# Two activation splits of the second feed-forward, queued behind the third copy of the next pair

## The chip, the cores and the metric

The kernel runs on one core of one Trainium2 chip. The metric is the device time of one execution in microseconds; the time of a kernel is the median of several runs. Shorter is better. TensorE is called PE below, VectorE DVE, ScalarE ACT, GpSimd POOL and SyncE SP, as the profile names them.

## The reference

The reference is one decoder layer on 512 tokens of width 1024. What the change touches is its last sub-layer, a gated feed-forward of width 2816:

```python
def swiglu(x, w_gate, w_up, w_down):
    return (jax.nn.silu(x @ w_gate) * (x @ w_up)) @ w_down

    f = swiglu(rms_norm(h, ffn2_norm_pre[l]), ffn2_w_gate[l], ffn2_w_up[l], ffn2_w_down[l])
    h = h + 0.5 * rms_norm(f, ffn2_norm_post[l])
```

The same feed-forward stands at the layer's beginning with other weights; between the two lie attention, a gated linear recurrence and an output product. All of it is float32.

## The kernel before

**Two halves of each number.** Every float32 operand of a product is split into a high and a low float32r part: ACT writes the high part (`split`, L302), DVE subtracts it from the source for the low part (L303). A product is then three matmuls, high by high, high by low and low by high (L729 to L731, in `seventh`). So each split is one ACT instruction and one DVE instruction that waits for it.

**Pairs and seven products.** The 2816 columns of gate and up are 22 blocks of 128. A pair is gate and up of one block. From block 3 on a pair is made by seven products of half-size matrices instead of eight (a Strassen-Winograd scheme); each product is 12 matmuls of 256 columns, so a pair is 84 matmuls. `seven_on` runs the products in the order p1, p5, p6, p2, p7, p3, p4 and sums on top of each other in PSUM: p6 is added onto p1 in the same bank `b`, p7 onto that. Between them the partial sum must be copied out of `b`, since the next product overwrites it. The copies are ACT instructions (`copy`, L743). There are four in a pair: the first after p1, the second (`c5`) after p5, the third (`c6`) after p6, and the fourth after p7. p7 may not write `b` until the third copy has read it, and p4 may not start until the fourth has written the bank that p4 adds to. The block's activation is then silu(gate) times up (L966 and L953 on ACT, L952, L957 and L962 on DVE).

**Parts.** Four blocks make a part. `into` gathers a part's four activations in the tile `tt` (one buffer), and makes the seven combinations that the product with the down weights needs; each is split into an `xf` tile, of which there are four buffers. At the fourth block of a part DVE forms the remaining sums in place in `tt` (L921, L927, L928), and four splits are made: p7, p5, then one of 1024 columns for p6 and p4 together, then one of 1024 columns for p2 and p3 together. These last two are what the change touches. The product of the part with the down weights (`down7`, L1046 to L1048) is done in four steps, one behind each of the next four pairs: p1 and p7, then p4 and p6, then p5, then p2 and p3.

**Order of the work.** The five engines run their own queues, each in its order. The order in a queue comes from a scheduler that goes by the order of the code and by priorities: work under `high_priority(offset=AHEAD)` (100) is put ahead of plain work, and work under `offset=EVAC` (200), such as the copies, ahead of that. `issue_after` keeps an instruction behind a named one. The splits of the next weights (`w_forms`, L691 to L696 for its sums, and `d_forms`, L988 to L1002) are made under `AHEAD` too, on the same two engines. Weights come by DMA from SP's queue into four `raw` buffers, each freed by the DVE subtraction that reads it last.

The second feed-forward has the parts of blocks 0 to 3, 4 to 7, 8 to 11 and 12 to 15, and a last one of six blocks without such splits. So the last splits of parts 1, 2 and 3 fall in the pairs of blocks 8, 12 and 16, all run by `seven_on`, and those of part 0 in the pair of block 4, run by the older form `seven`.

Of the kernel before, what the change touches and what calls it, by code (L numbers as in the profile page):

```python
# [12 lines left out]
AF = mybir.ActivationFunctionType  # L13
# [17 lines left out]
HB = 256  # L31
# [4 lines left out]
AHEAD = 100  # L36
# [147 lines left out]
def hybrid_layer(ctx: ExitStack, tc: tile.TileContext, xT: bass.AP, xN: bass.AP, wst: bass.AP,  # L184
                 first: bass.AP, rows: bass.AP, consts: bass.AP, bias: bass.AP, out: bass.AP):
    nc = tc.nc
    DVE, ACT, PE = nc.vector, nc.scalar, nc.tensor
# [44 lines left out]
    state = {"g": 0, "i": 0, "off": 0, "raw": None, "ahead": AHEAD, "split": None}  # L232
# [68 lines left out]
    def split(dh, dl, src):  # L301
        state["split"] = ACT.activation(dh, src, AF.Copy).ins  # L302
        state["low"] = DVE.tensor_sub(dl, src, dh.bitcast(F32)).ins  # L303

    def acc_ps():
        return psum.tile([P, T], F32, name="acc", tag="acc", bufs=5)
# [4 lines left out]
    def tmp(name):  # L311
        return tpool.tile([P, T], F32, name=name, tag="t")
# [39 lines left out]
    HALVES = (slice(0, HB), slice(HB, T))  # L352
# [369 lines left out]
    def seventh(t, w, p, ps, start):  # L722
        at = t[p].at
        if len(at(0, 0).shape) == 3:
            ps = ps.rearrange("q (b t) -> q b t", b=2)
        for k in range(4):
            ks = slice(k * P, (k + 1) * P)
            wh, wl, xh, xl = w[p][:, 0, ks], w[p][:, 1, ks], at(0, k), at(1, k)
            PE.matmul(ps, wh, xh, start=start and k == 0, stop=False, skip_group_check=True)  # L729
            PE.matmul(ps, wh, xl, start=False, stop=False, skip_group_check=True)  # L730
            state["product"] = PE.matmul(ps, wl, xh, start=False, stop=k == 3, skip_group_check=True).ins  # L731

    def seven_on(t, w, g0, g1, u0, u1):

        b, z, y, v = (acc_ps()[:, :HB] for _ in range(4))

        def copy(ps, dst=None):
            if dst is None:  # L740
                dst = tpool.tile([P, HB], F32, name="c", tag="c", bufs=CB)
            with tc.high_priority(offset=EVAC):
                state["copied"] = ACT.activation(dst, ps, AF.Copy).ins  # L743
            return dst

        seventh(t, w, "p1", b, True)
        copy(b, y)
        seventh(t, w, "p5", z, True)
        c5 = copy(z)
        seventh(t, w, "p6", b, False)  # L750
        c6 = copy(b)
        seventh(t, w, "p2", y, False)
        g0(y)
        seventh(t, w, "p7", b, False)
        copy(b, v)
        state["kept"] = state["copied"]
        u1(b, c5)
        seventh(t, w, "p3", z, False)
        g1(z, c6)
        seventh(t, w, "p4", v, False)  # L760
        u0(v)
# [62 lines left out]
        product("p4", o, False)  # L824
        fold(o, u[0], sign)

    def seven(t, w, z, g, u):


        b, y = acc_ps()[:, :HB], acc_ps()[:, :HB]  # L830

        def product(p, ps, start):
            seventh(t, w, p, ps, start)

        def copy(ps):
            c = tpool.tile([P, HB], F32, name="c", tag="c", bufs=CB)
            with tc.high_priority(offset=EVAC):
                ACT.activation(c, ps, AF.Copy)
            return c

        def sum_of(dst, ps, c):
            with tc.high_priority(offset=EVAC):
                DVE.tensor_add(dst, ps, c)

        product("p1", b, True)
        c1 = copy(b)
        product("p2", y, True)
        sum_of(g[0], y, c1)
        product("p6", b, False)
        c6 = copy(b)  # L850
        product("p5", z, True)
        c5 = copy(z)
        product("p7", b, False)
        c7 = copy(b)
        sum_of(u[1], c7, c5)
        product("p4", y, True)
        sum_of(u[0], y, c7)
        product("p3", z, False)
        sum_of(g[1], z, c6)

    def ffn(n, x, r, forms_x, apool, pss):
        t, steps = forms_x
        acts, sevens = {}, {}

        def f32r_big():
            return apool.tile([P, 4, T], F32R, name="xf", tag="xf", bufs=4)
# [1 line left out]
        def part_of(f):  # L868
            return next(a for a, (f0, f1) in enumerate(FF_PARTS) if f < f1)

        def act_at(f):

            a = part_of(f)
            i = f - FF_PARTS[a][0]
            if i == 0:
                acts[a] = apool.tile([P, 4, T], F32R, name="act4", tag="tt", bufs=1)
            elif i % 2 == 0:
                acts[a] = f32r_big()
            at, i = acts[a], i % 2
            acts["at", f] = at[:, 2 * i, :], at[:, 2 * i + 1, :]  # L880
            return acts["at", f]
# [7 lines left out]
        def into(f, put):  # L889

            a = part_of(f)
            if a not in SEVEN:
                u = tmp("u")
                put(u, lambda ap: ap)
                split(*act_at(f), u)
                return
            i = f - FF_PARTS[a][0]
            if i == 0:
                sevens[a] = {"tt": apool.tile([P, 4, 2, HB], F32, name="tt", tag="tt", bufs=1)}
            x = sevens[a]  # L900
            tt = x["tt"]
            put(tt[:, i // 2 * 2:i // 2 * 2 + 2, i % 2, :], lambda ap: ap.rearrange("p (q t) -> p q t", q=2))
            q = tt.rearrange("p q j t -> p q (j t)")

            def pair(*ps):
                v = f32r_big().rearrange("p (s c) t -> p s (c t)", s=2)
                for k, p in enumerate(ps):
                    x[p] = v[:, :, k * T:k * T + T]
                return v

            def form(v, src):
                split(v[:, 0], v[:, 1], src)


            if i == (1 if a else 3):
                pair("p1", "p7")
                form(x["p1"], q[:, 0])
                DVE.tensor_sub(q[:, 0], q[:, 0], q[:, 1])
            if i == 3:
                with tc.high_priority(offset=AHEAD):  # L920
                    DVE.tensor_sub(q[:, 1], q[:, 3], q[:, 1])  # L921
                    form(x["p7"], q[:, 1])
                    two = pair("p6", "p4")
                    v = f32r_big().rearrange("p c t -> p (c t)")
                    x["p5"] = v[:, 0:2 * T].rearrange("p (s t) -> p s t", s=2)
                    form(x["p5"], q[:, 0])
                    DVE.scalar_tensor_tensor(q[:, 0], q[:, 3], -1.0, q[:, 0], op0=ALU.mult, op1=ALU.subtract)  # L927
                    DVE.scalar_tensor_tensor(q[:, 1], q[:, 0], -1.0, q[:, 2], op0=ALU.mult, op1=ALU.subtract)  # L928
                    form(two, tt[:, 0:2].rearrange("p q j t -> p (q j t)"))
                    form(pair("p2", "p3"), tt[:, 2:4].rearrange("p q j t -> p (q j t)"))  # L930

        def std_out(psg, psu, f):

# [11 lines left out]
        def prod(f, w):  # L945
            g, u = tmp("g"), tmp("u")
            if f >= FIRST_ON[n]:
                lo, hi = HALVES

                def g1(z, c6):  # L950
                    with tc.high_priority(offset=EVAC):
                        DVE.tensor_add(g[:, hi], z, c6)  # L952
                    ACT.activation(g[:, hi], g[:, hi], AF.Silu)  # L953

                def u1(b, c5):
                    with tc.high_priority(offset=EVAC):
                        DVE.tensor_add(u[:, hi], b, c5)  # L957

                def u0(v):
                    def put(dst, view):  # L960
                        for q, (h, src) in enumerate(zip(HALVES, (v, u[:, hi]))):
                            DVE.scalar_tensor_tensor(dst[:, q] if len(dst.shape) == 3 else dst[:, h], g[:, h], -1.0,  # L962
                                                     src, op0=ALU.mult, op1=ALU.mult)
                    into(f, put)

                seven_on(t, w, lambda y: ACT.activation(g[:, lo], y, AF.Silu), g1, u0, u1)  # L966
                return
            seven(t, w, acc_ps()[:, :HB], [g[:, h] for h in HALVES], [u[:, h] for h in HALVES])
            ACT.activation(g, g, AF.Silu)
            into(f, lambda dst, v: DVE.scalar_tensor_tensor(dst, v(g), -1.0, v(u), op0=ALU.mult, op1=ALU.mult))  # L970

# [101 lines left out]
        for ev in ffn_order(n):  # L1073
            if ev[0] == "std":
                j = ev[1]
# [46 lines left out]
    u1 = act_of(*act_two(ap1))  # L1122
# [10 lines left out]
    for k in range(KC):  # L1133
        wh, wl, raw = wts[k]
        if k == 0:

            z = hm(0)
# [74 lines left out]
    with ExitStack() as mx:  # L1212
# [38 lines left out]
        def values_two(steps, then):  # L1251
# [78 lines left out]
            for j in range(2):  # L1330
# [4 lines left out]
        t, steps = forms_of(lambda i, j: Form(lambda s, k: um_t[2 * i + k // 2][:, s, k % 2, HALVES[j]]),  # L1335
                            apool, False, rec_half)
# [160 lines left out]
        two = []  # L1497
# [7 lines left out]
        for c in range(0, KC, 2):  # L1505
            g, u = tmp("g"), tmp("u")
            seven_wide(t, pair_of(("pair", 52 + c, 53 + c)), [g[:, h] for h in HALVES], [u[:, h] for h in HALVES],
                       then=gate)
# [3 lines left out]
        for c in range(KC):  # L1512
            ps = acc_ps()
            if c % 2 == 0:
                two = fetch(("attn", c))
# [3 lines left out]
    with ExitStack() as mx:  # L1519
# [151 lines left out]
        for i, (what, hd) in enumerate(LRU_ORDER):  # L1671
# [9 lines left out]
            def then():  # L1681
                if i + 1 < len(LRU_ORDER):
                    prepare(LRU_ORDER[i + 1])
# [189 lines left out]
```

## Time and profile before

| what | us |
|---|---|
| median of 3 runs | 1208.86 (1208.83 to 1209.17) |
| profiled execution, its own time | 1210.52 |
| its span, first to last instruction | 1208.7 |
| PE busy in it | 1200.0 |
| DVE busy in it | 1033.3 |
| ACT busy in it | 832.6 |

The pairs by seven products of the second feed-forward run from 899.7 to 1169.3 us of the span. A row of the chain or of the timeline begins with the start in us from the span's start, and the duration in us; the engine, the line of the kernel, and the tiles written and read follow. `x2` is a count of equal instructions in a row; a bracket at the end is the engine's idle time before, and what ended it. Matmuls and ACT and DVE instructions are pipelined: the next can start a little before the one before it has ended, so what an instruction costs its queue is the distance from its start to the next start.

### The profile page before, as it was taken

To read this page: it belongs to the slowest core of one execution; us is meant where nothing else is said; L and a number is where in the kernel's file an instruction comes from. 1 tells how busy PE (TensorE), PEld (TensorE's weight loads), DVE (VectorE), ACT (ScalarE), POOL (GpSimd) and SP (SyncE) were. 2 spreads that over 40 slices of the span, in tenths; PEclk is the share of its full clock that TensorE was granted. 3 is DMA by queue.
4 is the path that set the end of the run, shared out by engine and by line. 5 is a ranking of instruction groups with operands and counts; after the bars stand their busy time and mean duration, and the time that the engine had idled before them with its cause. 6 is when DMAs were issued, how large, how long until landed. Compare 5 with 4: busy or idle time off the path is not lost.

```text
span 1208.7 us, 18872 instructions
## 1 busy us (share of the span) xinstructions
PE 1200.0 (99%) x7222; PEld 1070.1 (89%) x7222; DVE 1033.3 (85%) x1626; ACT 832.6 (69%) x1447; POOL 26.1 (2%) x51
## 2 busy tenths in 40 slices
PE   9999999999999999999999999999999999999997
PEld 8889999999888888888888888888899999999996
DVE  7999888889689899999868899874898888889964
ACT  6566787887566576767736988734566677778763
POOL 0000000000011000000000000000100000000000
PEclk9999999999999999999999999999999999999999
DMA  7224343434625232222323432235443333343441
GB/s 267 88 92 124 135 139 106 140 111 153 247 102 163 71 97 96 88 75 92 111 66 120 163 122 99 85 108 191 141 140 105 123 123 124 121 128 118 140 175 70
DMA packets 45819, 149.77 MB, mean 124 GB/s; under 512 B 5152, under 2 KB 8608, under 8 KB 45728
## 3 DMA queue, kind: packets, MB, share of 16 engines
q1 hardware_dynamic: 38160, 131.09, 32.9%
q0 software_dynamic: 7280, 17.30, 4.3%
q8 instruction: 56, 0.92, 0.3%
q14 instruction: 35, 0.29, 0.1%
q10 hardware_dynamic: 288, 0.17, 0.0%
HBM read 138.06 MB, written 6.29 MB: 119 GB/s over the span
## 4 chain that ended last, share of the span: by engine, by line
PE 91%; DVE 4%; ACT 3%; issue 1%; DMA 1%; DVEq 0%; ACTq 0%
PE acc L729 9%; PE acc L780 9%; PE acc L731 9%; PE acc L730 9%; PE acc L315 7%; PE acc L317 7%; PE acc L316 7%; PE acc L781 5%; PE aux L1046 4%; PE aux L1047 4%; PE aux L1048 4%; PE acc L431 2%; PE acc L433 2%; PE acc L432 2%; DVE w L303 1%; ACT w L302 1%
## 5 line engine op out<-in xcount | busy, mean ns | idle before, releaser
L303 DVE TENSOR_TENSOR w<-raw,w 128x1024 fp32r<-128x1024 f32 (+1 forms) x272 | 296.7, 1098 | 36.3 <-ACT w L302 35.1
L302 ACT ACTIVATE w<-raw 128x1024 fp32r<-128x1024 f32 (+1 forms) x272 | 259.2, 958 | 84.3 <-PE acc L317 48.3
L729 PE MATMUL acc<-big,w 128*128 128x256 f32 x860 | 244.0, 284 | 0.2
L731 PE MATMUL acc<-big,w 128*128 128x256 f32 x860 | 243.4, 283 | 0.0
L730 PE MATMUL acc<-big,w 128*128 128x256 f32 x860 | 243.4, 283 | 0.0
L729 PEld LDWEIGHTS acc<-big,w 128*128 128x128 f32 x860 | 164.8, 192 | 2.8 <-ACT c L743 0.8
L730 PEld LDWEIGHTS acc<-big,w 128*128 128x128 f32 x860 | 164.8, 192 | 1.4
L731 PEld LDWEIGHTS acc<-big,w 128*128 128x128 f32 x860 | 164.8, 192 | 0.0
L780 PE MATMUL acc<-big,w 128*128 128x512 f32 x380 | 136.1, 397 | 0.3 <-DVE qk L804 0.3
L781 PE MATMUL acc<-big,w 128*128 128x256 f32 x380 | 107.3, 282 | 0.0
L1046 PE MATMUL aux<-w,xf 128*128 128x512 f32 x224 | 87.7, 391 | 0.1
L1047 PE MATMUL aux<-w,xf 128*128 128x512 f32 x224 | 87.5, 391 | 0.0
L1048 PE MATMUL aux<-w,xf 128*128 128x512 f32 x224 | 87.2, 389 | 0.0
L780 PEld LDWEIGHTS acc<-big,w 128*128 128x128 f32 x380 | 71.4, 188 | 16.4 <-PE acc L781 0.6
L781 PEld LDWEIGHTS acc<-big,w 128*128 128x128 f32 x380 | 71.7, 189 | 0.2
L303 DVE TENSOR_TENSOR w<-s,w 128x1024 fp32r<-128x1024 f32 x51 | 62.2, 1219 | 2.0 <-ACT w L302 1.6
L302 ACT ACTIVATE w<-s 128x1024 fp32r<-128x1024 f32 x51 | 54.0, 1059 | 8.8 <-PE acc L731 5.7
L315 PE MATMUL acc<-xf,w 128*128 128x512 f32 (+1 forms) x168 | 59.3, 355 | 0.0
L316 PE MATMUL acc<-xf,w 128*128 128x512 f32 (+1 forms) x168 | 58.7, 350 | 0.0
L317 PE MATMUL acc<-xf,w 128*128 128x512 f32 (+1 forms) x168 | 58.6, 349 | 0.0
L780 PE MATMUL acc<-rb,w 128*128 128x512 f32 x152 | 55.5, 397 | 0.0
L1048 PEld LDWEIGHTS aux<-w,xf 128*128 128x128 f32 x224 | 42.1, 188 | 8.9
(458 smaller groups left out, 2904.0 us busy)
## 6 DMA issues: line engine op xcount, KB each, us to landing
raw<-in_w SPq DMA_DIRECT2D x232, 512.0 KB, 3.5
big<-xf POOLq DMA_DIRECT2D x6, 512.0 KB, 3.3
gains<-in_rows POOLq DMA_DIRECT2D x5, 512.0 KB, 5.3
h<-in_x SPq DMA_DIRECT2D x8, 256.0 KB, 5.2
h<-in_xn POOLq DMA_DIRECT2D x4, 512.0 KB, 5.7
kept_m<-h POOLq DMA_DIRECT2D x4, 512.0 KB, 2.9
vals<-in_w SPq DMA_DIRECT2D x4, 512.0 KB, 6.1
h<-kept_m POOLq DMA_DIRECT2D x4, 512.0 KB, 6.2
```

The costliest lines, as they stand in the source:

```text
L302: state["split"] = ACT.activation(dh, src, AF.Copy).ins
L303: state["low"] = DVE.tensor_sub(dl, src, dh.bitcast(F32)).ins
L315: PE.matmul(ps, wh, xh, start=first, stop=False)
L316: PE.matmul(ps, wh, xl, start=False, stop=False)
L317: PE.matmul(ps, wl, xh, start=False, stop=last)
L729: PE.matmul(ps, wh, xh, start=start and k == 0, stop=False, skip_group_check=True)
L730: PE.matmul(ps, wh, xl, start=False, stop=False, skip_group_check=True)
L731: state["product"] = PE.matmul(ps, wl, xh, start=False, stop=k == 3, skip_group_check=True).ins
L780: PE.matmul(part, wh, at(BOTH, k), start=start and k == 0, stop=False, skip_group_check=True)
L781: last = PE.matmul(cross, wl, at(0, k), start=False, stop=k == 3, skip_group_check=True)
L1046: PE.matmul(ps, xh, wh, start=first and j == 0, stop=False, skip_group_check=True)
L1048: PE.matmul(ps, xl, wh, start=False, stop=j == 1, skip_group_check=True)
```

## The change

The last two splits of a part are no longer made at the end of `into`. They are put into a function `rest`, which the second feed-forward keeps in a list `later`. The next pair calls it (`then()`) just behind its third copy, and there it stands under `issue_after` of that copy: neither split may be queued ahead of it. In the first feed-forward `rest` is called at once, as before.

```diff
-    def seven_on(t, w, g0, g1, u0, u1):
+    def seven_on(t, w, g0, g1, u0, u1, then=lambda: None):
...
         seventh(t, w, "p6", b, False)
         c6 = copy(b)
+        then()
         seventh(t, w, "p2", y, False)
...
-    def seven(t, w, z, g, u):
+    def seven(t, w, z, g, u, then=lambda: None):
...
         c6 = copy(b)
+        then()
         product("p5", z, True)
...
     def ffn(n, x, r, forms_x, apool, pss):
         t, steps = forms_x
-        acts, sevens = {}, {}
+        acts, sevens, later = {}, {}, []
+
+        def forms_left():
+            while later:
+                later.pop()()
...
                     DVE.scalar_tensor_tensor(q[:, 1], q[:, 0], -1.0, q[:, 2], op0=ALU.mult, op1=ALU.subtract)
-                    form(two, tt[:, 0:2].rearrange("p q j t -> p (q j t)"))
-                    form(pair("p2", "p3"), tt[:, 2:4].rearrange("p q j t -> p (q j t)"))
+                    last = pair("p2", "p3")
+
+                def rest():
+                    with tc.high_priority(offset=AHEAD), tc.issue_after(state["copied"]) if n == 2 else nullcontext():
+                        form(two, tt[:, 0:2].rearrange("p q j t -> p (q j t)"))
+                        form(last, tt[:, 2:4].rearrange("p q j t -> p (q j t)"))
+
+                if n in (2,):
+                    later.append(rest)
+                else:
+                    rest()
...
-                seven_on(t, w, lambda y: ACT.activation(g[:, lo], y, AF.Silu), g1, u0, u1)
+                seven_on(t, w, lambda y: ACT.activation(g[:, lo], y, AF.Silu), g1, u0, u1, forms_left)
                 return
-            seven(t, w, acc_ps()[:, :HB], [g[:, h] for h in HALVES], [u[:, h] for h in HALVES])
+            seven(t, w, acc_ps()[:, :HB], [g[:, h] for h in HALVES], [u[:, h] for h in HALVES], forms_left)
```

What this does to the queues is shown for the pair of block 8; the pairs of blocks 12 and 16 are changed in the same way. First ACT's queue, from the end of the part's third-last split. `c<-acc` are the second and third copy, `xf<-tt` the two splits, `w<-sum` a split of the down weights, `w<-raw` one of the next pair's weights, `acc<-acc` the fourth copy. Before:

```order
L1034 ACTIVATE aux<-ea 128x512
L743 ACTIVATE c<-acc 128x256
L302 ACTIVATE xf<-tt 128x1024
L743 ACTIVATE c<-acc 128x256
L302 ACTIVATE xf<-tt 128x1024
L302 ACTIVATE w_9753<-sum 128x1024
L302 ACTIVATE w_9764<-raw 128x1024
L743 ACTIVATE acc<-acc 128x256
L966 ACTIVATE g<-acc 128x256
```

and with the change (lines of the feed-forward have moved down by some 15, and the numbers in the weights' names differ):

```order
L1049 ACTIVATE aux<-ea 128x512
L743 ACTIVATE c<-acc 128x256 x2
L302 ACTIVATE w_9749<-sum 128x1024
L302 ACTIVATE xf<-tt 128x1024
L302 ACTIVATE w_9760<-raw 128x1024
L743 ACTIVATE acc<-acc 128x256
L302 ACTIVATE xf<-tt 128x1024
L981 ACTIVATE g<-acc 128x256
```

The third copy now stands right behind the second. The first of the two splits has gone behind the third copy and behind a weight split, the second behind the fourth copy.

DVE's queue in the same pair: `xf<-tt` are the low parts of the two splits, `s`, `raw` and `w` belong to the weights of the next pair (block 9), `u` and `g` are the sums of this pair's activation. Before:

```order
L928 TENSOR_SCALAR tt<-tt 128x512
L303 TENSOR_TENSOR xf<-tt,xf 128x1024 x2
L303 TENSOR_TENSOR w_9753<-sum,w_9753 128x1024
L957 TENSOR_TENSOR u<-acc,c 128x256
L952 TENSOR_TENSOR g<-acc,c 128x256
L691 TENSOR_TENSOR s_9760<-raw 128x512
L303 TENSOR_TENSOR w_9764<-raw,w_9764 128x1024
L692 TENSOR_TENSOR s_9760<-s_9760,raw 128x512
L693 TENSOR_TENSOR raw<-raw 128x512
L696 TENSOR_TENSOR raw<-s_9760,raw 128x512
L993 TENSOR_TENSOR sum<-sum,raw 128x1024
L303 TENSOR_TENSOR w_9765<-s_9760,w_9765 128x1024
```

and with the change:

```order
L934 TENSOR_SCALAR tt<-tt 128x512
L303 TENSOR_TENSOR w_9749<-sum,w_9749 128x1024
L691 TENSOR_TENSOR s_9756<-raw 128x512
L303 TENSOR_TENSOR xf<-tt,xf 128x1024
L692 TENSOR_TENSOR s_9756<-s_9756,raw 128x512
L972 TENSOR_TENSOR u<-acc,c 128x256
L967 TENSOR_TENSOR g<-acc,c 128x256
L693 TENSOR_TENSOR raw<-raw 128x512
L303 TENSOR_TENSOR w_9760<-raw,w_9760 128x1024
L303 TENSOR_TENSOR w_9761<-s_9756,w_9761 128x1024
L696 TENSOR_TENSOR raw<-s_9756,raw 128x512
L303 TENSOR_TENSOR xf<-tt,xf 128x1024
```

The weight subtraction and two of the next pair's sums have moved ahead of the low part of the first split; the low part of the second has gone behind two of the next pair's weight subtractions. PE's, POOL's and SP's queues hold the same instructions in the same order as before. In the pair of block 4, where part 0's two splits fall, ACT's order is the same as before, and on DVE the low part of one weight split (`w<-s`) has moved ahead of theirs.

## The prediction

> **What bounds the kernel now.** The page first: which engine fills the span, and what ends PE's idle time.
>
> ```profile
> span 1208.7 us, 18872 instructions
> PE 1200.0 (99%) x7222; PEld 1070.1 (89%) x7222; DVE 1033.3 (85%) x1626; ACT 832.6 (69%) x1447; POOL 26.1 (2%) x51
> ```
>
> PE is busy for 99% of the span, so a change that only reorders ACT and DVE can gain no more than what PE waits for them in the stage that it touches. How much that is, the windows show: start, end and length of a stretch, then busy time and count by engine, the granted clock in front of the last two columns. The first three stretches are the pairs of blocks 8, 12 and 16, from their first matmul to the first one behind them; the fourth is the pair of block 9, which holds the same 84 matmuls and none of the part's splits; the fifth is the stretch ahead.
>
> ```profile
> 969.22:979.86 10.64, 10.56 (x85) 10.17 (x84) 9.38 (x14) 8.76 (x16) 0.00 (x0) 1.00 0.48 148
> 1029.22:1039.86 10.64, 10.56 (x85) 10.16 (x84) 9.10 (x13) 8.77 (x16) 0.00 (x0) 1.00 0.49 148
> 1089.22:1099.86 10.64, 10.56 (x85) 10.16 (x84) 9.10 (x13) 8.77 (x16) 0.00 (x0) 1.00 0.48 146
> 985.33:995.40 10.07, 10.07 (x86) 10.07 (x84) 7.51 (x12) 7.63 (x15) 0.00 (x0) 1.00 0.44 158
> 880.00:969.00 89.00, 89.00 (x649) 84.72 (x648) 79.65 (x104) 58.27 (x89) 0.93 (x2) 1.00 0.38 119
> ```
>
> The three pairs take 10.64 us each and the plain one 10.07: 0.57 us more in each, 1.71 in all. In the 89 us ahead PE has no idle time that the view resolves. The busy sum hides most of the loss (10.56 of 10.64), because a matmul after a wait is shown longer; the lengths are what counts.
>
> The chain of waits says where the 0.57 us go. It leaves PE once in each of these pairs and comes back by the third copy.
>
> ```profile
> 973.10 0.70 DVE tt L928
> 973.85 0.94 issue
> 974.79 0.38 ACT c L743
> 975.21 0.39 PE acc L729
> 978.34 0.37 PE acc L729
> ...
> 1034.80 0.38 ACT c L743
> ...
> 1094.80 0.38 ACT c L743
> ```
>
> The piece called issue, 973.85 to 974.79, is what the chain can't name; ACT's timeline, below, shows a split of `tt` there. PE's rows of the pair of block 8 show the two steps out of rhythm: a matmul of 256 columns starts 0.12 us after the one before it (975.43 to 975.55 and so on in a plain run), but here
>
> ```profile
> 974.85 0.28 PE L731 MATMUL acc<-big,w 128*128 128x256 f32 x1
> 975.21 0.39 PE L729 MATMUL acc<-big,w 128*128 128x256 f32 x1
> 975.43 0.28 PE L730 MATMUL acc<-big,w 128*128 128x256 f32 x1
> ...
> 978.06 0.28 PE L731 MATMUL acc<-big,w 128*128 128x256 f32 x1
> 978.32 0.39 PE L729 MATMUL acc<-big,w 128*128 128x256 f32 x1
> 978.54 0.28 PE L730 MATMUL acc<-big,w 128*128 128x256 f32 x1
> ```
>
> p7 starts at 975.21 instead of 974.97, and its second matmul comes 0.22 later instead of 0.12: 0.24 + 0.10 = 0.34 us. p4 starts at 978.32 instead of 978.18, and again 0.10 is lost behind it: 0.24 us. Together 0.58, which agrees with the 0.57 of the windows. ACT's queue gives the reason for both.
>
> ```profile
> 972.43 0.39 ACT L743 ACTIVATE c<-acc 128x256 f32<-128x256 f32 x1
> 973.83 1.06 ACT L302 ACTIVATE xf<-tt 128x1024 fp32r<-128x1024 f32 x1 [1.01 <-DVE tt L928]
> 974.79 0.37 ACT L743 ACTIVATE c<-acc 128x256 f32<-128x256 f32 x1
> 975.05 1.05 ACT L302 ACTIVATE xf<-tt 128x1024 fp32r<-128x1024 f32 x1
> 976.01 1.05 ACT L302 ACTIVATE w<-sum 128x1024 fp32r<-128x1024 f32 x1
> 976.95 1.05 ACT L302 ACTIVATE w<-raw 128x1024 fp32r<-128x1024 f32 x1
> 977.90 0.37 ACT L743 ACTIVATE acc<-acc 128x256 f32<-128x256 f32 x1
> 978.20 0.37 ACT L966 ACTIVATE g<-acc 128x256 f32<-128x256 f32 x1
> ```
>
> ACT idles 1.01 us for DVE's `tt` (L928), then makes the split, and the third copy stands behind both; so p7 waits. The fourth copy stands behind three pieces of work of 1024 columns and ends at 978.27, 0.05 us ahead of p4's start; so p4 waits.
>
> **The change, ACT's side.** When could the third copy start? In the plain pair it waits for PE alone:
>
> ```profile
> 985.31 0.64 ACT L302 ACTIVATE w<-raw 128x512 fp32r<-128x512 f32 x1
> ...
> 987.26 0.40 ACT L743 ACTIVATE acc<-acc 128x256 f32<-128x256 f32 x1
> ...
> 989.84 0.39 ACT L743 ACTIVATE c<-acc 128x256 f32<-128x256 f32 x1 [0.33 <-PE acc L731]
> ...
> 988.20 0.28 PE L729 MATMUL acc<-tx,w 128*128 128x256 f32 x1
> ...
> 991.08 0.28 PE L729 MATMUL acc<-big,w 128*128 128x256 f32 x1
> ```
>
> The copy starts 1.24 us ahead of p7's first matmul (991.08) and ends 0.85 ahead of it. In the pair of block 8 p7 is due at 974.97, so the copy runs from 973.73 to 974.12 and p7 doesn't wait: 0.34 us less. ACT is free for it: the second copy ended at 972.82, and what it idled for is behind it now. From there I walk the new queue by the distances of the rows above, 0.30 us for a copy that has work behind it (977.90 to 978.20) and 0.95 for 1024 columns (975.05, 976.01, 976.95, 977.90). `w<-sum` starts at 974.03, the first split at 974.98 (its source is ready at 973.79, the end of L928), `w<-raw` at 975.93, the fourth copy at 976.88, and it ends at 977.25. Without the first wait p4 is due at 974.97 + 24 x 0.12 = 977.85. It is ready 0.60 ahead: the second wait goes too, 0.24 us less. The number of splits ahead of the fourth copy behind the third is the same three minus one, since one of the two has gone behind it.
>
> The second split then takes 977.18 to 978.23, and the gate's silu (L966) follows at about 978.13, where it was at 978.20. Nothing is lost for it.
>
> **DVE's side.** DVE's rows of before, from the low parts of the splits to the weights for the next step of the down product:
>
> ```profile
> 974.92 2.44 DVE L303 TENSOR_TENSOR xf<-tt,xf 128x1024 fp32r<-128x1024 f32 x2 [1.13 <-ACT xf L302]
> 977.28 1.22 DVE L303 TENSOR_TENSOR w<-sum,w 128x1024 fp32r<-128x1024 f32 x1
> 978.41 0.42 DVE L957 TENSOR_TENSOR u<-acc,c 128x256 f32<-128x256 f32 x1
> 978.75 0.41 DVE L952 TENSOR_TENSOR g<-acc,c 128x256 f32<-128x256 f32 x1
> ...
> 983.76 1.22 DVE L303 TENSOR_TENSOR w<-s,w 128x1024 fp32r<-128x1024 f32 x1
> ...
> 986.72 0.41 DVE L962 SCALAR_TENSOR_TENSOR tt<-g,acc 128x256 f32<-128x256 f32 x1
> ...
> 987.42 1.23 DVE L303 TENSOR_TENSOR w<-raw,w 128x1024 fp32r<-128x1024 f32 x1
> ```
>
> The distances are 1.14 us for 1024 columns, 0.60 for 512 (estimate, half of it and a start), 0.33 for 256 (978.41 to 978.75). In the new order `w<-sum` must wait for ACT's part, which ends at 974.03 + 1.05 = 975.08, so DVE idles from 973.79 to 975.12, 0.2 us longer than now. Then `s` 976.26, the first split's low part 976.86, `s` 978.00, `u` 978.60, `g` 978.94, `raw` 979.27, the two weight subtractions 979.87 and 981.01, `raw` 982.15, the second split's low part 982.75. From then on the same work is left as in the old order, and it ends within 0.1 us of 988.65, where the last row above ends. The next pair now starts 0.57 us sooner, at 984.76. Its first weights were due then and have been ready since 981.1; the second ones (983.76 plus 1.22 before, 981.01 plus 1.22 now) come 2.7 us earlier for a need that moves by 0.57. So on DVE the change costs nothing that shows. What hides it is the lead of the weights, 2 us or more; were it gone, each late microsecond would be a PE microsecond.
>
> The two splits themselves are not needed soon: p6 and p4 of the part meet their weights behind the next pair (995.40 in the windows' fourth row), p2 and p3 two pairs after that. The tile `tt` has one buffer and is written next at 986.72 in the old order; in the new one its last reader ends at 982.75 + 1.22 = 983.97, so this costs 0.
>
> SP's queue is the same. Its loads wait for `raw` buffers that DVE frees, and in the walk those are freed at about the same time or up to a microsecond earlier. A load lands 4.4 us after its issue in this stretch, and the weights that PE needs are split well before. Cost 0, at worst what the rival below says. The pair of block 4 has the old order on ACT and no wait of PE in the 89 us shown, so 0 both ways.
>
> **The sum.** Three times 0.57 us = 1.71 us. PE has no other idle time behind these pairs, so the end moves by as much. Against the profiled execution: 1210.52 - 1.71 = 1208.81, in its span 1208.7 - 1.7 = 1207.0. The median of the runs, 1208.86, is 1.66 below the profiled execution; the same 1.71 off the median gives 1207.15, and I say 1207.2. The bounds of the unknown: if only the first wait goes, 3 x 0.34 = 1.0 us; if neither goes, 0.
>
> A rule is weighed here. The Trainium skill, "Perfetto Trace Analysis", Optimization Strategy, says that the same gap repeating on the engine that should be saturated can mean that there aren't enough buffers for the next tile. By it the gap would belong to the PSUM bank that p6, p7 and the copy share, a new order would leave it where it is, and the time would stay at 1208.9. The plain pair speaks against it: with the same bank and the same copies, p7 finds the copy done 0.85 us ahead.
>
> **The rivals.**
>
> *The waits stay (same bank).* The copy would be late for another reason than the split, and p7 and p4 wait as now: 1208.9. For it speaks that the wait is on a shared bank in all three pairs; against it the 0.85 us of the plain pair.
>
> *Only p7's wait goes.* If `w<-raw`, now ahead of the fourth copy, stood for its DMA or for the buffer that p2 reads, the fourth copy would be 0.6 us or more late: 1208.86 - 1.0 = 1207.8. Against it: the split ran back to back with its neighbours at 976.95, and I have it only one microsecond earlier.
>
> *More than the waits.* Executions differ: the profiled one and the median lie 1.66 us apart. If such a difference falls on the good side, or the earlier second weights remove something that the views don't resolve, the time is 1206.4 or less, around 1205.9. The change's own rows give no such term.
>
> *Slower: the next pair's third product waits.* The sums that DVE makes for the next pair's last weights (`raw`, L693 and L696) now stand behind one or three subtractions of 1024 columns, and ACT's splits `w<-raw` of 1024 and 512 columns wait for them, with the seeds of the down product and the first copy of the next pair queued behind. ACT came to the split of 512 at 985.31; now it comes at 984.2 by the walk, 0.57 for PE's lead and the rest because a split `w<-s` has moved into an idle stretch of ACT. p6 of that pair waits for this copy; in the old order it was ready 988.20 - (987.26 + 0.40) = 0.54 us ahead. In the walk L696 is done by 982.8, 1.4 us before ACT asks. So DVE must slip by 1.4 + 0.5 = 1.9 us, nearly two subtractions, before PE loses anything; each microsecond beyond costs 3 in the sum. To end 0.2% slower it needs (2.4 + 1.7) / 3 = 1.4 more, a slip of 3.3 us; at 3.5 the time is 1208.86 - 1.7 + 3 x 1.6 = 1212.0. DVE is busy 9.38 of 10.64 us in this pair but 7.51 of 10.07 in the next, which speaks for a slip that is caught up.
>
> **How the numbers follow.** Both waits go: 0.64. Only p7's: 0.07. Neither: 0.08. More than the waits: 0.13. The next pair waits: 0.08. A change of 0.2% is 2.4 us, about what a measurement of this kernel can tell from none; the first three cases lie within it, so same 0.79, faster 0.13, slower 0.08. The likeliest gives 1207.2. Its own range is 1206.6 to 1207.7, from the 0.34 us between the runs shown on either side and 0.2 for the walk. The range for 8 in 10 takes in the cases up to no change and a part of the faster one: 1206.2 to 1209.0.
>
> **What would show it.** Right: the pairs of blocks 8, 12 and 16 take 10.07 us like the plain one; no matmul starts more than 0.12 us behind the last; the third copy starts 1.06 us ahead of where it was (974.79 to 973.73), straight behind PE; the chain of waits stays on PE from 876 us to the tail, without L743. Wrong: PE rows of 0.39 us at a `tx` product of the next pair, or ACT rows of `w<-raw` idle before for DVE's L693 or L696; or the copy still late with something else ahead of it.

## The result

The changed kernel takes 1207.51 us (median of 21 runs, 1206.85 to 1209.73) against 1209.04 us for the kernel before in the same job (21 runs, 1208.49 to 1209.85). The ratio is 0.9986, with a 95% interval of 0.9981 to 0.9992: 1.0 to 2.3 us less, 1.53 by the medians. It is faster, by less than the 0.2% that the prediction called no change. The lines of the feed-forward stand about 15 further down in the changed kernel, and each kernel of the experiments has line numbers of its own; the names of the tiles are the same in all.

The first lines of the page of the kernel after:

```profile
span 1206.1 us, 18869 instructions
PE 1197.7 (99%) x7222; PEld 1070.1 (89%) x7222; DVE 1032.8 (86%) x1626; ACT 833.2 (69%) x1447; POOL 26.1 (2%) x51
```

The same windows as in the prediction: the pairs of blocks 8, 12 and 16, the plain pair of block 9, and the stretch ahead.

```profile
968.26:978.34 10.08, 10.08 (x86) 10.07 (x85) 8.64 (x14) 8.33 (x15) 0.00 (x0) 1.00 0.47 156
1027.70:1037.78 10.08, 10.08 (x86) 10.07 (x85) 8.37 (x13) 8.33 (x15) 0.00 (x0) 1.00 0.46 154
1087.14:1097.21 10.07, 10.07 (x85) 10.06 (x84) 8.36 (x13) 8.33 (x15) 0.00 (x0) 1.00 0.49 155
983.80:993.88 10.08, 10.08 (x86) 10.07 (x85) 8.11 (x13) 7.04 (x14) 0.00 (x0) 1.00 0.46 158
879.00:968.04 89.04, 89.04 (x649) 84.77 (x647) 79.70 (x104) 58.28 (x89) 0.77 (x2) 1.00 0.38 118
```

The three pairs are as short as the plain one, and PE is busy for all of their length. ACT's rows in the pair of block 8 show what moved. The profile of after stands 0.96 us earlier here than that of before (968.26 against 969.22 at the pair's start), so 972.78 is 973.74 on the old axis.

```profile
972.78 0.38 ACT L743 ACTIVATE c<-acc 128x256 f32<-128x256 f32 x1 [0.92 <-PE acc L731]
973.06 1.05 ACT L302 ACTIVATE w<-sum 128x1024 fp32r<-128x1024 f32 x1
974.00 1.05 ACT L302 ACTIVATE xf<-tt 128x1024 fp32r<-128x1024 f32 x1
974.95 1.05 ACT L302 ACTIVATE w<-raw 128x1024 fp32r<-128x1024 f32 x1
975.90 0.37 ACT L743 ACTIVATE acc<-acc 128x256 f32<-128x256 f32 x1
976.20 1.04 ACT L302 ACTIVATE xf<-tt 128x1024 fp32r<-128x1024 f32 x1
```

The third copy is released by PE (the bracket: idle 0.92 us, ended by PE's `acc`), no longer by DVE's `tt` through a split. On PE the two matmuls that came late before, the first of p7 and the first of p4, stand in the rhythm of 0.12 us:

```profile
973.89 0.28 PE L731 MATMUL acc<-big,w 128*128 128x256 f32 x1
974.01 0.28 PE L729 MATMUL acc<-big,w 128*128 128x256 f32 x1
...
976.77 0.28 PE L731 MATMUL acc<-big,w 128*128 128x256 f32 x1
976.90 0.28 PE L729 MATMUL acc<-big,w 128*128 128x256 f32 x1
```

The spans of the two profiles differ by 2.6 us, more than the medians do. Followed matmul by matmul, PE's lead grows by 0.56 to 0.57 us in each of the three pairs, 1.69 in all, and the chain of waits of the new profile stays on PE from 876 to 1158 us. The other 0.95 arises ahead of the pairs, in code that is the same: PE gains 0.62 us between 102 and 113 us, in the first feed-forward, and 0.43 in small steps between 420 and 727 us, after it had lost 0.10 at the start. Ahead of the first of these places DVE waits for the same load in both profiles, first before, then after:

```profile
97.38 0.69 DVE L692 TENSOR_TENSOR s<-s,raw 128x512 f32<-128x512 f32 x1 [1.77 <-DMA raw<-in_w]
```

```profile
96.81 0.69 DVE L692 TENSOR_TENSOR s<-s,raw 128x512 f32<-128x512 f32 x1 [1.05 <-DMA raw<-in_w]
```

The load of 512 KB took 5.8 us from issue to landing in the profile of before and 5.1 in that of after. In the chain of waits of before this load leads over DVE and a weight split on ACT to PE's late matmul at 102.41 us. The ten profiles of this document, those of the experiments included, bear it out: where DVE waits 0.35 to 1.05 us for the load (seven profiles), the same hundred matmuls of PE around this place take 15.86 us; where it waits 1.77 (before), 2.10 (the kernel with three passes) and 2.29 us (the one without the edge), they take 16.47, 16.82 and 17.08. So PE's step comes with the late load; no run changed the time of the load alone. The profiled execution of before was 1.66 us above its median, so a comparison of these two profiles alone would have said 2.6 us.

### The profile page after: what moved, and what is told of

It is laid out like the page before. It is cut to its first block, busy times and chain, and to the rows that moved or that the text cites. A ratio compares the mean times of both kernels' runs of the same rounds, so it can differ in the third digit from the quotient of the medians.

```text
span 1206.1 us, 18869 instructions
## 1 busy us (share of the span) xinstructions
PE 1197.7 (99%) x7222; PEld 1070.1 (89%) x7222; DVE 1032.8 (86%) x1626; ACT 833.2 (69%) x1447; POOL 26.1 (2%) x51
## 4 chain that ended last, share of the span: by engine, by line
PE 96%; DVE 2%; ACT 1%; issue 0%; DMA 0%; DVEq 0%; ACTq 0%
PE acc L729 10%; PE acc L731 10%; PE acc L730 10%; PE acc L781 9%; PE acc L315 7%; PE acc L317 7%; PE acc L316 7%; PE acc L782 5%; PE aux L1061 4%; PE aux L1062 4%; PE aux L1063 4%; PE acc L433 2%; PE acc L431 2%; PE acc L432 2%; PE aux L433 1%; PE aux L432 1%
## 5 line engine op out<-in xcount | busy, mean ns | idle before, releaser
L303 DVE TENSOR_TENSOR w<-sum,w 128x1024 fp32r<-128x1024 f32 x24 | 29.4, 1224 | 25.9 <-ACT w L302 25.9
```

## The experiments

All ran beside the kernel before. It took 1209.04 us (33 runs) in the job of four of them: both splits straight behind the copy, no edge, three pieces ahead, four pieces between. It took 1209.18 us (21 runs) in the job of the other four: three and four pieces again with PE's order held, and the two with passes on DVE. A difference to the change is the difference to the kernel before in the same job plus the 1.53 us by which the change is faster. The first question was whether ACT's order is the cause, and which part of the change does it.

**Both splits straight behind the third copy.** Now neither a weight split nor the fourth copy stands between them:

```diff
-                    with tc.high_priority(offset=AHEAD), tc.issue_after(state["copied"]) if n == 2 else nullcontext():
+                    with tc.high_priority(offset=EVAC), tc.issue_after(state["copied"]) if n == 2 else nullcontext():
```

> Both splits stand directly behind the third copy on ACT, ahead of the weight split, and DVE's queue is the one of the kernel before (both low parts ahead of the weights). ACT's order (the prediction's theory): the third copy finds ACT free, three pieces of 1024 columns lie between it and the fourth copy, which ends 0.6 us ahead of p4; the three pairs take 10.07 us and the time is 1.7 us below the kernel before, like the change. DVE's order (rival: the gain comes from the next pair's weights, which the change put ahead on DVE): the pairs stay at 10.64 us and the time at that of before. Same bank (rival): 10.64 us as well.

Measured: 1207.45 us (11 runs), ratio 0.9986 (0.9978 to 0.9995), the same as the change. The pair of block 8 in the windows, and ACT's rows:

```profile
967.53:977.61 10.08, 10.08 (x86) 10.07 (x85) 8.64 (x13) 8.34 (x16) 0.00 (x0) 1.00 0.46 153
```

```profile
972.05 0.38 ACT L743 ACTIVATE c<-acc 128x256 f32<-128x256 f32 x1 [0.92 <-PE acc L731]
972.33 2.00 ACT L302 ACTIVATE xf<-tt 128x1024 fp32r<-128x1024 f32 x2
974.23 1.05 ACT L302 ACTIVATE w<-sum 128x1024 fp32r<-128x1024 f32 x1
975.17 0.37 ACT L743 ACTIVATE acc<-acc 128x256 f32<-128x256 f32 x1
```

Three pieces of 1024 columns stand between the copies, as in the change, and which three they are makes no difference. The order of DVE's queue, which the change moved a good deal and this kernel hardly, has no part in the gain.

**The code moved, without the edge.** The splits are called at the new place, but nothing keeps them behind the copy:

```diff
-                    with tc.high_priority(offset=AHEAD), tc.issue_after(state["copied"]) if n == 2 else nullcontext():
+                    with tc.high_priority(offset=AHEAD):
```

> The change without the edge that keeps the splits behind the third copy. ACT's queue then has the first split ahead of the third copy as in the kernel before, and the second one still behind it, ahead of the fourth copy; on DVE the second low part is behind the next pair's weights as in the change. ACT's order: p7 waits 0.34 us as before, and three pieces lie between third and fourth copy as before, so p4 waits 0.24: pairs 10.64 us, time as before. DVE's order: most of the gain, pairs near 10.1 us, 1 to 1.7 us below before.

Measured: 1209.27 us (11 runs), ratio 1.0001 (0.9992 to 1.001): no change from before. Pair of block 8 in the windows, and ACT's rows:

```profile
969.55:980.20 10.65, 10.57 (x86) 10.17 (x84) 9.38 (x14) 8.42 (x16) 0.00 (x0) 1.00 0.45 142
```

```profile
974.16 1.06 ACT L302 ACTIVATE xf<-tt 128x1024 fp32r<-128x1024 f32 x1 [1.01 <-DVE tt L934]
975.12 0.37 ACT L743 ACTIVATE c<-acc 128x256 f32<-128x256 f32 x1
975.39 1.05 ACT L302 ACTIVATE w<-sum 128x1024 fp32r<-128x1024 f32 x1
```

The second split has gone behind the two weight splits here, but the first is still ahead of the copy, and ACT idles 1.01 us for `tt` as before. So the whole 0.57 us of a pair hangs on that one split ahead of the third copy. The PSUM bank, the copies and the products are the same in this kernel, in the one above and in the change, and the wait is there only with the split ahead. With that the rival of the shared bank falls. The Trainium skill, "Perfetto Trace Analysis", Optimization Strategy, says that such a repeated gap can mean too few buffers; here it did not: no buffer was added, and the gap went.

**Three pieces ahead of the copy.** If ACT's queue sets the start of p7, more work ahead of the copy must lengthen the wait by just that work. In the kernel before, the first split's high part is written twice, and the copy is held behind both splits; what is computed stays the same:

```diff
-        c6 = copy(b)
+        with tc.issue_after(state.pop("hold")) if "hold" in state else nullcontext():
+            c6 = copy(b)
...
+                    if n == 2 and a:
+                        ACT.activation(two[:, 0], tt[:, 0:2].rearrange("p q j t -> p (q j t)"), AF.Copy)
...
+                    if n == 2 and a:
+                        state["hold"] = state["split"]
```

> The kernel before, with the high part of the first split written twice in parts 1 to 3 and the third copy held behind the splits, so that three pieces of 1024 columns stand ahead of it instead of one. ACT's order: the copy starts 2 x 0.95 = 1.9 us later, at 976.7 on the time axis of before, p7 at 977.1 instead of the due 974.97; the fourth copy is then early enough. Pairs 10.07 + 2.1 + 0.1 = 12.3 us, time 3 x 1.66 = 5.0 us above before. Same bank, or DVE's order: the pairs hardly move from 10.64.

Measured: 1211.12 us (10 runs), ratio 1.0019 (1.001 to 1.0028). That is 2.1 us more than before, not 5.0. ACT's rows are as walked; PE's show what was not:

```profile
974.36 0.28 PE L731 MATMUL acc<-big,w 128*128 128x256 f32 x1
975.17 0.39 PE L729 MATMUL acc<-big,w 128*128 128x256 f32 x1 [0.54 <-ACT c L743]
```

p7 starts right behind the copy, but the matmuls before it run until 974.36 instead of about 972.9: the scheduler had put the 12 matmuls of p3 (1.44 us) ahead of p7. So the miss would be the price of a wait that PE's order had filled by more than half. That was a theory after the fact, so it was tested.

**The same, with PE's products held in their order:** p3 behind p7, p4 behind p3, and the next pair's p1 behind p4.

```diff
-        seventh(t, w, "p3", z, False)
+        with tc.issue_after(state["product"]) if pin else nullcontext():
+            seventh(t, w, "p3", z, False)
```

> The kernel before, with the high part of the first split written twice in blocks 8, 12 and 16 and the third copy held behind both splits, so that three pieces of 1024 columns stand ahead of the copy where one stood; and PE's products of these pairs are held in the written order, which the scheduler had altered in the run without this hold. If ACT's queue ahead of the copy is what p7 waits for and nothing fills the wait: the copy starts 2 x 0.95 = 1.91 us later, p7 waits 0.24 + 1.91 and 0.10 behind it, p4 no longer waits (its copy is ready 0.8 us ahead), so a pair takes 10.07 + 2.25 = 12.3 us instead of 10.64, and the time is 1209.0 + 3 x 1.67 = 1214.0 us. If the copy is late because of the PSUM bank and not because of ACT's queue: 10.64 us a pair and 1209.0. If PE's other order was not the reason why the run without this hold lost only 2.1 us: again about 1211.1.

Measured: 1215.25 us (5 runs, 1213.59 to 1215.82), ratio 1.0045 (1.0033 to 1.0058), 4.0 to 7.0 us more than before; the walk said 5.0. Pair of block 8 in the windows; ACT's rows; PE's rows:

```profile
967.33:979.62 12.29, 10.33 (x85) 10.12 (x84) 10.08 (x15) 9.71 (x16) 0.00 (x0) 1.00 0.42 129
```

```profile
971.93 1.06 ACT L937 ACTIVATE xf<-tt 128x1024 fp32r<-128x1024 f32 x1 [1.00 <-DVE tt L935]
972.89 1.99 ACT L302 ACTIVATE xf<-tt 128x1024 fp32r<-128x1024 f32 x2
974.79 0.36 ACT L743 ACTIVATE c<-acc 128x256 f32<-128x256 f32 x1
```

```profile
972.96 0.28 PE L731 MATMUL acc<-big,w 128*128 128x256 f32 x1
975.20 0.39 PE L729 MATMUL acc<-big,w 128*128 128x256 f32 x1 [1.96 <-ACT c L743]
```

Two more pieces ahead of the copy make the pair 1.65 us longer (12.29 against 10.64): 1.90 more at p7, less the 0.24 at p4, which is no longer late. So the pair fits the walk: three times 1.65 is 5.0 us. The time fits less well: the median lies 1.2 above the walk's 1214.0, within the interval. The profiled execution, 1213.59, is the fastest of the five, and what makes the others longer the profile of one can't show.

**Four pieces between the third copy and the fourth.** The change stays, but the fourth copy is held behind the second split:

```diff
-        copy(b, v)
+        with tc.issue_after(state.pop("hold")) if "hold" in state else nullcontext():
+            copy(b, v)
...
+                        if n == 2 and a:
+                            state["hold"] = state["split"]
```

> The change, with only the fourth copy held behind the second split, so that four pieces of 1024 columns lie between the third and the fourth copy instead of three. ACT's order: p7 does not wait; the fourth copy runs from 977.83 to 978.20 on the axis of before, p4 is due at 977.85 and starts at 978.25, with 0.10 lost behind it: pairs 10.57 us, time 1.5 us above the change, so about that of before. If the 0.60 us of lead that the walk gives the fourth copy in the change were wrong, the loss would differ from 0.5 us per pair by as much.

Measured: 1207.88 us (10 runs), ratio 0.999 (0.9981 to 0.9999), 0.4 us above the change where 1.5 was expected. The reason is again PE's order:

```profile
976.28 0.28 PE L729 MATMUL acc<-big,w 128*128 128x256 f32 x1
976.40 0.28 PE L730 MATMUL acc<-big,w 128*128 128x256 f32 x1
976.65 0.39 PE L729 MATMUL acc<-big,w 128*128 128x256 f32 x1
```

The first two rows are the next pair's p1, put ahead of p4; p4 is due at 976.28 and starts at 976.65, late by 0.37 us (the walk: 0.40), but PE has 0.24 of them filled. With the 0.10 behind the wait a pair loses 0.23 in this profile, 0.7 us in three.

**The same, with PE's products held in their order,** by the same lines as above:

> The changed kernel with the fourth copy held behind the second split in blocks 8, 12 and 16 (four pieces of 1024 columns between the third copy and the fourth, not three), and PE's products held in the written order. By the walk of ACT's queue the third copy starts at 972.78 in the changed kernel's trace, the four pieces at 973.06, 974.00, 974.95 and 975.90, the fourth copy at 976.85, and it ends at 977.23; p4 is due at 976.90 and so starts 0.38 us late, with 0.10 behind it: 10.55 us a pair, 3 x 0.48 = 1.4 us more than the changed kernel, 1208.9 us. If the fourth copy has more lead than the 0.62 us that I read: 10.07 a pair and 1207.5.

Measured: 1208.69 us (11 runs), ratio 0.9995 (0.9986 to 1.0004), 0.5 us less than before where the change has 1.5: 1.0 us above the change, 1.4 expected. Windows, ACT and PE of the pair of block 8:

```profile
967.46:977.99 10.53, 10.31 (x85) 10.11 (x84) 9.08 (x14) 8.73 (x15) 0.00 (x0) 1.00 0.47 147
```

```profile
971.97 0.38 ACT L743 ACTIVATE c<-acc 128x256 f32<-128x256 f32 x1 [0.91 <-PE acc L731]
...
976.04 0.37 ACT L743 ACTIVATE acc<-acc 128x256 f32<-128x256 f32 x1
```

```profile
975.97 0.28 PE L731 MATMUL acc<-big,w 128*128 128x256 f32 x1
976.46 0.39 PE L729 MATMUL acc<-big,w 128*128 128x256 f32 x1 [0.22 <-ACT acc L743]
```

p4 starts 0.37 us late (0.49 behind the last matmul instead of 0.12), and the pair is 0.45 us longer than in the change; the walk said 0.48. So the lead of the fourth copy in the change, 0.62 us, is real, and one more piece of 0.95 uses it up.

**How much slip DVE can take.** The slower rival had a price: 1.9 us of slip free, three for each one behind that. The changed kernel gets idle passes on DVE in the weights of blocks 9, 13 and 17:

```diff
+            for _ in range(3 if key in (("gu", 2, 9), ("gu", 2, 13), ("gu", 2, 17)) else 0):
+                DVE.tensor_tensor(ur, ur, ur, op=ALU.min)
             split(a[:, 0, :], a[:, 1, :], gr)
```

> The changed kernel with three more passes of 1024 columns on DVE (the minimum of a tile with itself, which changes nothing) in the weights of blocks 9, 13 and 17; PE's order is the same. Three passes are 3 x 1.17 = 3.5 us of slip. By the prediction's price for the slower rival (1.9 us of slip are free, each microsecond behind that costs three in the sum): 1207.5 + 3 x 1.6 = 1212.3 us. By a walk of the new queues in the changed kernel's trace: the third pass ends at 985.3, ACT's split for p7 and p4 runs from there to 986.3, the next pair's first copy behind it ends at 986.65, and p6 of that pair is due at 986.67; the low part of p7's weights is ready at 988.2 and due at 989.8: nothing is lost, 1207.5 to 1207.7 us.

Measured: 1212.03 us (10 runs, 1209.94 to 1213.99), ratio 1.0019 (1.001 to 1.0028), 2.9 us more than before and so 4.4 more than the change. The profiled execution, 1213.99, is the slowest of the ten, so its rows show more loss than the median has. The old price (4.8) has the size and my walk (0 to 0.2) has not; but the place is neither's. The pair of block 9 takes 10.08 us after the change (shown above), and the stretch from its end to the pair of block 12

```profile
993.88:1027.70 33.82, 33.82 (x230) 31.43 (x229) 28.98 (x41) 26.79 (x46) 0.00 (x0) 1.00 0.43 126
```

In a window each, the same two with three passes:

```profile
984.28:994.77 10.49, 10.41 (x85) 10.16 (x84) 10.03 (x14) 7.23 (x13) 0.00 (x0) 1.00 0.44 150
994.77:1030.34 35.57, 34.47 (x231) 31.56 (x229) 30.15 (x42) 26.72 (x47) 0.00 (x0) 1.00 0.37 120
```

The pair of block 9 loses 0.41 us, 0.10 of it at p6, where the rival and the walk had looked and the walk had the copy just in time, nothing at p7, and the rest at p4. The sum L698 (the old L696), at which the rival had put the slip, is not late in this pair: it starts at 981.63 us, where the changed kernel has it (981.15, with the 0.49 us between the two profiles at this place). What the passes delay is the split behind the third of them and DVE's low parts. The pairs behind it lose 1.75 more. ACT's rows there name what hands the slip on:

```profile
1007.09 1.06 ACT L302 ACTIVATE w<-raw 128x1024 fp32r<-128x1024 f32 x1 [1.10 <-DMA raw<-in_w]
...
1009.27 0.37 ACT L745 ACTIVATE acc<-acc 128x256 f32<-128x256 f32 x1
1012.30 0.63 ACT L302 ACTIVATE w<-raw 128x512 fp32r<-128x512 f32 x1 [2.65 <-DVE raw L698]
```

A weight split waits 1.10 us for its load, whose buffer DVE would have had to free, and the fourth copy behind it is 0.68 us late for p4; then ACT waits for DVE's sum (L698), and the next pair's first copy is 0.73 late. This last wait is the rival's mechanism, two pairs behind the place that it had named. The load was issued at 1001.20 us, 0.03 behind the end of a DVE subtraction that reads a `raw` buffer (999.95 to 1001.17), and took 5.9 us; the changed kernel issues it at 998.01, about 2.3 us sooner by PE's rhythm, and there it took 4.5. So the trace fits a buffer that came free late; no run tested it alone.

**Five passes, with PE's products of these pairs held in their order:**

> As the kernel with three passes, but with five (5.8 us of slip), and with PE's products of these pairs held in the written order. By the prediction's price: 1207.5 + 3 x (5.8 - 1.9) = 1219 us. By the walk of the queues: the last pass ends at 989.4 in the changed kernel's trace, the high part of the weights of p7 and p4 is ready on ACT at 990.5 and the low part on DVE at 992.1; p7 of the next pair is due at 989.55 with the high part and at 989.8 with the low one, so 2.3 to 2.4 us are lost in each of three pairs: 1207.5 + 7 = 1214.5 us. If the weights have a lead that neither counts: 1207.5.

Measured: 1220.09 us (4 runs), ratio 1.009 (1.0076 to 1.0103), 10.9 us more than before and 12.4 more than the change; the old price said 11.5, the walk 7. The same two windows:

```profile
983.40:995.68 12.28, 10.59 (x85) 10.18 (x84) 12.28 (x16) 7.55 (x13) 0.00 (x0) 1.00 0.36 114
995.68:1030.83 35.15, 34.09 (x231) 31.48 (x229) 30.24 (x42) 26.71 (x46) 0.00 (x0) 1.00 0.38 126
```

At the place walked, p7 of block 9 and its weights, the loss is 2.20 us, where the walk had 2.3 to 2.4; behind it come 1.33 us that the walk left out since it stopped there. In the whole stretch behind the first passes PE's matmuls fall 12.8 us behind those of the change, 6.6 of it at the place walked and some 1.4 at the lower clock of the last section. So a walk of one pair is right for the place walked and no bound for the time: DVE, busy for 12.28 of 12.28 us here, takes the rest of the slip into the following pairs.

## Why the prediction was right

- *The sum, three times 0.57.* Right: the three pairs went from 10.64 to 10.07 or 10.08 us, and PE's lead grew by 0.56 to 0.57 in each, 1.69 against the 1.71 forecast. The medians' 1.53 lies 0.18 below the forecast, and their interval of 1.0 to 2.3 us holds it. So 21 runs of each kernel told 1.5 us from no change, where the prediction had taken 2.4 for about the least that can be told. The predicted 1207.2 lies 0.3 below the measured 1207.51, of which 0.18 is the changed baseline (1209.04 in this job, 1208.86 in the runs shown).
- *ACT's walk.* Right to 0.02 us once the 0.96 us between the profiles is taken off: the third copy was forecast for 973.73 and stands at 973.74, `w<-sum` for 974.03 (974.02), the first split 974.98 (974.96), `w<-raw` 975.93 (975.91), the fourth copy 976.88 (976.86). The lead ahead of p4 was forecast as 0.60 us and is 0.62; the held fourth copy shows that it is no more. One sentence of the prediction miscounts ("the same three minus one"): three pieces of 1024 columns stand between the third copy and the fourth before and after, as its own walk has them. p4's wait goes because the third copy, and with it the three pieces, starts 1.05 us sooner while p4 is due only 0.33 sooner.
- *DVE's walk.* Right where it was walked. DVE idles 1.31 us for `w<-sum`, where the walk had 1.33 and before had 1.13 (for the first split); the first split's low part follows at 976.84 (forecast 976.86), L696 at 982.11 (982.15), the second split's low part at 982.71 (982.75). Of the next pair's sums only one (L691) has moved ahead of the first split's low part, as the walk has it, not two as the text on the change says; L692 stands behind it. These rows of after show the walk:

```profile
974.14 1.23 DVE L303 TENSOR_TENSOR w<-sum,w 128x1024 fp32r<-128x1024 f32 x1 [1.31 <-ACT w L302]
...
975.88 1.22 DVE L303 TENSOR_TENSOR xf<-tt,xf 128x1024 fp32r<-128x1024 f32 x1
...
981.15 0.69 DVE L696 TENSOR_TENSOR raw<-s,raw 128x512 f32<-128x512 f32 x1
981.75 1.23 DVE L303 TENSOR_TENSOR xf<-tt,xf 128x1024 fp32r<-128x1024 f32 x1
```

- *The waits stay (the bank).* Fell, by the kernel without the edge and the one with both splits straight behind the copy.
- *Only p7's wait goes.* Fell: p4 is in rhythm in all three pairs.
- *More than the waits.* The two profiles differ by 0.95 us more than the waits, but in unchanged code ahead of the pairs; the medians show no such gain.
- *The next pair waits.* It didn't. With 3.5 us of slip the time was forecast as 1212.0, and it is 1212.03 with three passes. That agreement is luck: the price stood for a slip of the sums and a loss at p6 of the next pair; in the run the sums of that pair are not late, p6 loses 0.10, and the loss comes at p4 and in the pairs behind. So a slip of the sums alone was not run, and its price stays open. "A slip that is caught up" is the half-sentence that failed: two more pairs later it is not. The change itself makes DVE late by 0.2 us in the walk; the next pair's first copy ends at 986.06 in its profile and p6 starts at 986.67, so it had 0.61 us to spare and this cost nothing.

## What to carry to other kernels

When an engine waits for a short copy, look at what stands ahead of the copy in its own queue and what that is waiting for; work that nobody needs before the end of the next pair belongs behind it, and how much fits ahead of the next copy is counted in pieces (here three of 0.95 us fit and four don't). Moving the code did nothing here; only the edge that forbids the old order did. When an experiment delays an instruction under a scheduler that orders all engines, hold the other engines' order, or it measures the scheduler's answer too: 2.1 us instead of 6.1, and 0.4 instead of 1.0.

## What was not expected of the hardware

With five passes, PE loses 2.2 us at p7 in the pairs of blocks 9, 13 and 17 alike. Once, behind the second of these, the granted clock fell, while behind the first and the third it stayed at 1.00. Windows of 4 us behind the second and the first (the granted clock is the third number from the end):

```profile
1054.50:1058.70 4.20, 4.20 (x23) 4.20 (x24) 3.21 (x4) 1.89 (x4) 0.00 (x0) 0.60 0.69 212
991.60:995.60 4.00, 4.00 (x34) 4.00 (x35) 4.00 (x7) 2.19 (x5) 0.00 (x0) 1.00 0.71 213
```

At a clock of 0.60 PE ran 23 matmuls of 256 columns in 4.20 us, where 35 fit at 0.12: 1.4 us lost. The share of the DMA engines was the same, 0.69 and 0.71 (0.70 behind the third), so that alone doesn't bring it on. Three waits of one profile don't show what does.
